# Gated units of a hybrid decoder block: gate and up of 2304 columns with the weights stationary and x moving

## Chip, core and metric

The kernel runs on one core of one Trainium2 chip. The metric is the time of one execution on the device, in microseconds. Three runs of the kernel before took 1052.83 us in the median (1052.79 to 1053.9). One more execution was recorded by the hardware profiler; its trace and its page are what the profile rows below come from.

## The reference

Two layers work on 256 tokens of 1024 columns in float32. Each layer has four sublayers, and each sublayer is normed before and after:

```python
for i in range(DEPTH):                       # 2
    f = swiglu(rmsnorm(h, g[0]), ffn_gate[i, 0], ffn_up[i, 0], ffn_down[i, 0])
    h = h + 0.5 * rmsnorm(f, g[1])
    mix = hybrid_mixer(rmsnorm(h, g[2]), ...)
    h = h + rmsnorm(mix, g[3])
    f = swiglu(rmsnorm(h, g[4]), ffn_gate[i, 1], ffn_up[i, 1], ffn_down[i, 1])
    h = h + 0.5 * rmsnorm(f, g[5])
    gate = jax.nn.sigmoid(rmsnorm(h, g[6]) @ w_ple_gate[i])
    h = h + rmsnorm((p[i] @ w_ple[i]) * gate, g[7])

def swiglu(x, w_gate, w_up, w_down):         # 1024 -> 2816 -> 1024
    return (jax.nn.silu(x @ w_gate) * (x @ w_up)) @ w_down
```

The change is in `swiglu`, which is computed four times. These are the four gated units; "unit 1" is the first of layer 0, "unit 2" the second of layer 0, and units 3 and 4 are those of layer 1.

## The kernel before

**Precision.** Every float32 operand of a product is split into two parts of 12 significant bits, hi and lo, and a product is three matmuls: hi by hi, hi by lo, lo by hi. For x the parts lie in `xh`, `xl`, transposed (columns of x on the partitions), one tile of each for each of the two token tiles t of 128 tokens.

**Weights.** The class `Weights` streams them in the order of their use. SP issues one load of 1 MB for each raw tile; there are four raw buffers, and the next load is issued when a raw tile is used up. A raw tile holds two pieces of 1024 columns. `prepare` splits a piece: ACT copies it to hi (L152), then DVE subtracts hi from the raw piece and writes lo (L153). There are ten slots for such pairs of hi and lo, two of them lent to the mixer while it runs. Where the splits stand among the other instructions is set by `PLAN`: `run` emits a phase of matmuls and, at the steps named there ("ticks"), one split each; other pieces of work are inserted at steps of their own. Every engine works in the order in which it is written here; the only planner is this table.

**A gated unit** (`ffn`) goes through the 2816 hidden columns in chunks of 512, 512, 256, 512, 512, 512. For a chunk there are six phases: gate of token tiles 0 and 1, up of 0 and 1, down of 0 and 1. In gate and up the parts of x are the stationary operand and the weights move, 512 columns at a time (L321 to L323), so tokens come out on the partitions, and the norm's factor of x, `rx`, is a number per partition. ACT makes the silu with that factor as its scale (L448). DVE makes (up times rx) times silu (L453). The product `hm` has tokens on the partitions, but down needs the hidden columns there: TensorE transposes four blocks of it (`hid_t`, L398), ACT copies the result to hi (L401) and DVE subtracts to lo (L402). Down (L479) then adds into four banks of PSUM that are kept for it (`accs`: two token tiles by two halves of the 1024 columns). All other products and transposes use a second pool of four banks in turn. In the last chunk the down phases go by halves of the columns, and `begin_post` and `post` form the norm of the result, which goes into the residual stream h and, normed and transposed, into x of the next sublayer.

**Beside this.** `setup_late` loads and builds masks and rotary tables for the mixer: four DMAs of SP from L292 on, a chain on DVE from L296 on, two sines on ACT (L308, L312). It is written once, behind the first chunk's down phases of unit 1. `extra` transposes the per-layer inputs p (`split_p`), in units 2 and 4, ahead of the last down phases.

Of the kernel before, what the change touches and what calls it, by code (L numbers as in the profile page):

```python
# [9 lines left out]
F32 = mybir.dt.float32  # L10
# [4 lines left out]
ALU = mybir.AluOpType  # L15
# [22 lines left out]
CHUNKS = [(0, 512), (512, 512), (1024, 256), (1280, 512), (1792, 512), (2304, 512)]  # L38
# [58 lines left out]
class Weights:  # L97
    """Streams the weights in the order of their use: one load per raw tile, which is then
    split into pieces hi + lo = w, each of 12 significant bits."""

    def __init__(self, nc, raw_pool, slots):
        """slots: pairs of (pool, tag, columns) for hi and lo; those of self.shut are taken by others."""
        self.nc, self.raw_pool, self.slots = nc, raw_pool, slots
        self.free = list(range(len(slots)))
        self.shut = set()
        self.slot = {}
        self.specs = []
        self.loads = []
        self.raw = {}
        self.got = {}  # L110
        self.next = 0
        self.next_load = 0

    def add(self, keys, src, a, n):
        load = len(self.loads)
        self.loads.append((src, a * len(keys), n))
        for i, key in enumerate(keys):
            self.specs.append((key, load, i, a, n, i == len(keys) - 1))
# [22 lines left out]
    def prepare(self):  # L141
# [3 lines left out]
        raw = self.raw[load][:, part * a : (part + 1) * a, :]  # L145
# [30 lines left out]
def hybrid_block(ctx: ExitStack, tc: tile.TileContext, a, out):  # L176
# [60 lines left out]
    for l in range(DEPTH):  # L237
        for f in range(2):
# [21 lines left out]
            for c, (f0, w) in enumerate(CHUNKS):  # L260
                ka = 1024 // w
                for name, src in (("G", wg), ("U", wu)):
                    for j in range(KD // (2 * ka)):
                        W.add([(l, f, c, name, 2 * j), (l, f, c, name, 2 * j + 1)],
                              src[:, 2 * ka * j : 2 * ka * (j + 1), f0 : f0 + w], ka, w)
                for j in range(w // 256):
                    k0 = f0 // P + 2 * j
                    W.add([(l, f, c, "D", 2 * j), (l, f, c, "D", 2 * j + 1)], wd[:, k0 : k0 + 2, :], 1, 1024)
# [20 lines left out]
    def setup_late():  # L289
        """Masks and rotary tables."""  # L290
# [25 lines left out]
    xh = [keep.tile([P, KD, P], F32R, name=f"xh{t}") for t in range(T)]  # L316
    xl = [keep.tile([P, KD, P], F32R, name=f"xl{t}") for t in range(T)]

# [6 lines left out]
    def run(gen, name, *fns):  # L325
        """Emits a phase of matmuls, with fns and splits of weights at the steps that PLAN has for it."""
# [15 lines left out]
    def rstd(ss, ns, tag="rs", eps=EPS):  # L342
        """(ss / n + eps) ** -0.5 for each column of ss."""
# [16 lines left out]
    def begin_post(t, f, gain, q):  # L360
        """For the first half of the columns: their part in f's norm, and f * gain. The norm's factor
        comes out divided by q."""
        e = sum_sq([f[0]])
        nc.gpsimd.tensor_scalar(e[:, 0:1], e[:, 0:1], q * q / D, q * q * EPS, op0=ALU.mult, op1=ALU.add)
        y = k2("y")
        nc.vector.tensor_tensor(y, f[0], gain[:, :512], op=ALU.mult)
        part[t] = e, y

    def post(t, f, gain, q, gain_pre):
        """h[t] += norm(f) / q; gives h[t] * gain_pre, and what does the second half of the columns."""  # L370
        e, y0 = part[t]
        r = rstd(sum_sq([f[1]]), [D / (q * q)], eps=e[:, 0:1])
        y1 = k2("y")
        nc.vector.tensor_tensor(y1, f[1], gain[:, 512:], op=ALU.mult)
# [32 lines left out]
    def proj(ps, t, keys, fin, cols=None, k0=0, first=True, last=True, sh=None, sl=None, lo_last=False):  # L407
        """ps += x[t] @ w over the pieces named by keys."""
# [24 lines left out]
    def ffn(l, f, pend, gain_post, gain_pre, extra=lambda: None):  # L433
        """pend: emits the transposes of x that are still to come. Gives the same for what follows."""
        hidden = work.tile([P, T, 2, 4, P], F32R, tag="k8", name="hid")
        hid = [(hidden[:, t, 0], hidden[:, t, 1]) for t in range(T)]
        sg = {}
        accs = {}

        def gkeys(c, name):  # L440
            return [(l, f, c, name, j) for j in range(4 if CHUNKS[c][1] == 512 else 2)]

        def gate(t, c, *fns, lo_last=False):
            w = CHUNKS[c][1]
            ps = bank("g")
            run(proj(ps[:, :w], t, gkeys(c, "G"), t == 1, lo_last=lo_last), f"{kind}.G{t}", *fns)
            s = k2("silu")
# [462 lines left out]
```

## Time and profile before

| | before |
|---|---|
| runs: median of three (lowest to highest) | 1052.83 us (1052.79 to 1053.9) |
| profiled execution, from the first to the last instruction | 1052.4 us |
| mean granted clock of TensorE (1 is full speed) | 0.999 |
| TensorE matmul busy | 1037.1 us |
| VectorE (DVE) busy | 645.8 us |
| ScalarE (ACT) busy | 528.9 us |
| GpSimd (POOL) busy | 51.1 us |
| DMA | 189.02 MB, mean 180 GB/s |

In the profile, PE is TensorE's matmul and PEld its weight load, SPq the queue of DMA issues of SyncE. A row of a timeline gives the start of a group of instructions in us from the span's start, its length, the engine, the line, the operation, the tiles (result, then sources), the shape, and how many instructions it holds; in brackets the idle time of the engine ahead of it and what ended that. A row of the costliest groups gives the number of instructions, their busy time, the mean ns of one, the engine's idle time ahead of them and its causes. Matmuls overlap in a trace, so the sum of their durations says less than the distance between two starts.

### The profile page before, as it was taken

The numbers are of one execution on the slowest core, as the hardware profiler recorded it, in microseconds if no ns is written. First come the engines' busy times: TensorE is split into PE (matmuls) and PEld (weight loads), VectorE is DVE, ScalarE is ACT, GpSimd is POOL, SyncE is SP. The second block draws the span as 40 slices with busy tenths as digits, with TensorE's granted clock in tenths as the row PEclk, the third lists the DMA queues.
The fourth block names the chain that finished last, engine by engine and source line by source line (L and its number), as shares of the span: only waits on it lengthen the run. The fifth ranks groups of instructions, "written<-read, shape, count | busy, mean of one in ns | idle before, by whom it ended". The sixth has DMA issues, their size and how long they took to land.

```text
span 1052.4 us, 13069 instructions
## 1 busy us (share of the span) xinstructions
PE 1037.1 (99%) x5168; PEld 867.0 (82%) x5168; DVE 645.8 (61%) x819; ACT 528.9 (50%) x744; POOL 51.1 (5%) x123
## 2 busy tenths in 40 slices
PE   8999999999999999999999999999999999999997
PEld 5889888878888898888878888888888888988886
DVE  4765554778677455456776545557877864555474
ACT  5544443555556444444665444445564654444463
POOL 0000000210020000000110000002000200000011
PEclk9999999999999999999999999999999999999999
DMA  8864546364227564554547645455532575545601
GB/s 321 304 227 168 193 164 211 106 222 160 82 94 272 191 213 160 201 200 160 200 160 259 212 169 200 153 163 168 180 120 82 190 275 184 198 162 172 227 21 40
DMA packets 86158, 189.02 MB, mean 180 GB/s; under 512 B 3665, under 2 KB 15313, under 8 KB 86098
## 3 DMA queue, kind: packets, MB, share of 16 engines
q1 hardware_dynamic: 86098, 188.20, 52.0%
q8 instruction: 40, 0.66, 0.2%
q14 instruction: 20, 0.16, 0.0%
HBM read 187.13 MB, written 1.05 MB: 179 GB/s over the span
## 4 chain that ended last, share of the span: by engine, by line
PE 92%; DVE 3%; ACT 2%; DMA 1%; issue 1%; POOL 0%; SPq 0%; DVEq 0%; POOLq 0%; ACTq 0%
PE acc L479 23%; PE u L323 8%; PE u L321 8%; PE u L322 8%; PE g L321 7%; PE g L323 7%; PE g L322 7%; PE tp L398 3%; PE o L706 2%; PE sc L666 1%; DVE lo L153 1%; PE gt L323 1%; PE gt L322 1%; PE gt L321 1%; PE f L321 1%; PE f L323 1%
## 5 line engine op out<-in xcount | busy, mean ns | idle before, releaser
L153 DVE TENSOR_TENSOR lo<-raw,hi 128x1024 fp32r<-128x1024 f32 (+1 forms) x338 | 405.1, 1214 | 204.2 <-ACT hi L152 194.1
L152 ACT ACTIVATE hi<-raw 128x1024 fp32r<-128x1024 f32 (+1 forms) x338 | 347.2, 1049 | 170.9 <-PE u L323 79.3
L479 PE MATMUL acc<-hi,hid 128*128 128x512 f32 x704 | 201.5, 392 | 0.0
L479 PEld LDWEIGHTS acc<-hi,hid 128*128 128x128 f32 x704 | 131.7, 188 | 27.4
L321 PE MATMUL u<-hi,xh 128*128 128x512 f32 (+1 forms) x384 | 145.3, 379 | 0.0
L323 PE MATMUL u<-hi,xl 128*128 128x512 f32 (+1 forms) x384 | 143.2, 373 | 0.0
L322 PE MATMUL u<-lo,xh 128*128 128x512 f32 (+1 forms) x384 | 143.0, 372 | 0.0
L321 PE MATMUL g<-hi,xh 128*128 128x512 f32 (+1 forms) x360 | 135.0, 375 | 2.3 <-ACT xh L401 2.3
L323 PE MATMUL g<-hi,xl 128*128 128x512 f32 (+1 forms) x360 | 134.6, 374 | 0.0
L322 PE MATMUL g<-lo,xh 128*128 128x512 f32 (+1 forms) x360 | 134.5, 374 | 0.0
L479 PE MATMUL acc<-lo,hid 128*128 128x512 f32 x352 | 118.3, 395 | 0.0
L323 PEld LDWEIGHTS u<-hi,xl 128*128 128x128 f32 x384 | 72.3, 188 | 13.0
L322 PEld LDWEIGHTS u<-lo,xh 128*128 128x128 f32 x384 | 72.4, 188 | 12.1
L321 PEld LDWEIGHTS u<-hi,xh 128*128 128x128 f32 x384 | 72.3, 188 | 12.0
L321 PEld LDWEIGHTS g<-hi,xh 128*128 128x128 f32 x360 | 68.5, 190 | 14.4 <-ACT xh L401 2.7
L322 PEld LDWEIGHTS g<-lo,xh 128*128 128x128 f32 x360 | 68.5, 190 | 12.3 <-DVE lo L153 0.5
L323 PEld LDWEIGHTS g<-hi,xl 128*128 128x128 f32 x360 | 68.4, 190 | 12.4 <-DVE xl L402 0.6
L479 PEld LDWEIGHTS acc<-lo,hid 128*128 128x128 f32 x352 | 66.2, 188 | 13.2
L401 ACT ACTIVATE hid<-tp 128x512 fp32r<-128x512 f32 (+1 forms) x48 | 27.0, 563 | 95.6 <-PE tp L398 95.6
L453 DVE SCALAR_TENSOR_TENSOR hm<-u,rs,silu 128x512 f32<-128x512 f32 (+1 forms) x48 | 33.7, 703 | 65.1 <-PE u L323 65.1
L448 ACT ACTIVATE silu<-g,rs 128x512 f32<-128x512 f32 (+1 forms) x48 | 31.3, 652 | 81.3 <-PE g L323 81.2
L402 DVE TENSOR_TENSOR hid<-tp,hid 128x512 fp32r<-128x512 f32 (+1 forms) x48 | 31.0, 647 | 44.0 <-ACT hid L401 43.6
(216 smaller groups left out, 1195.0 us busy)
## 6 DMA issues: line engine op xcount, KB each, us to landing
raw<-in_ffn_up SPq DMA_DIRECT2D x44, 1024.0 KB, 5.1
raw<-in_ffn_down SPq DMA_DIRECT2D x44, 1024.0 KB, 5.0
raw<-in_ffn_gate SPq DMA_DIRECT2D x43, 1024.0 KB, 5.2
raw<-in_w_in SPq DMA_DIRECT2D x12, 1024.0 KB, 5.2
raw<-in_w_out SPq DMA_DIRECT2D x8, 1024.0 KB, 5.1
raw<-in_w_ple_gate SPq DMA_DIRECT2D x8, 1024.0 KB, 5.1
gain<-in_norm_gains SPq DMA_DIRECT2D x15, 512.0 KB, 4.0
raw<-in_w_in SPq DMA_DIRECT2D x4, 832.0 KB, 5.2
```

Source lines behind the costliest of these rows:

```text
L152: self.nc.scalar.activation(hv, raw, AF.Copy)
L153: self.nc.vector.tensor_tensor(lv, raw, hv.bitcast(F32), op=ALU.subtract)
L321: nc.tensor.matmul(ps, sh, wh, start=first, stop=False)
L322: nc.tensor.matmul(ps, sh, wl, start=False, stop=False)
L323: nc.tensor.matmul(ps, sl, wh, start=False, stop=last)
L398: nc.tensor.transpose(ps[:, j * P : (j + 1) * P], src[:, (b0 + j) * P : (b0 + j + 1) * P], ident)
L401: nc.scalar.activation(hv, v, AF.Copy)
L402: nc.vector.tensor_tensor(dl[:, k0 + b0 : k0 + b0 + nb, :], v, hv.bitcast(F32), op=ALU.subtract)
L448: nc.scalar.activation(s[:, :w], ps[:, :w], AF.Silu, scale=rx[t][:, 0:1])
L453: nc.vector.scalar_tensor_tensor(hm[:, :w], ps[:, :w], rx[t][:, 0:1], sg[t][:, c0 : c0 + w], op0=ALU.mult, op1=ALU.mult)
L479: nc.tensor.matmul(accs[t][n], hid[t][x][:, b, :], ws[w][:, 0, n * 512 : (n + 1) * 512], start=first and x + w == 0, stop=final and x == 1)
L706: nc.tensor.matmul(dst, pt[:, b * P : (b + 1) * P], va[:, kb, hd, :], start=kb == 0, stop=kb == t)
```

## The change

The first 512 columns of each unit stay as they were, except that `hm` is now up times silu without `rx`. Both factors of x are left out on the up side; the post norm takes them in (`by`, through `times` and the scale of the sum of squares).

The other 2304 columns, 18 blocks (b = 4 to 21) of 128, are computed transposed. The four parts of x (hi of token tiles 0 and 1, lo of 0 and 1) become one tile `x4`, so that they can move as one row of 512 columns. `block` takes one block of weight columns: for each of the eight k tiles, the hi part of the weights is stationary and all of `x4` moves (512 columns), then the lo part is stationary and hi of x moves (256 columns). The first half of the bank then holds hi by hi plus lo by hi, the second hi by lo. `both` adds the halves: ACT copies the second to SBUF, DVE adds the first. The hidden columns are now on the partitions, as down needs them: the transposes of `hm` are gone in these blocks, and `rx` is a number per column there. `factors` spreads it over all partitions, once for each unit: two fills of ACT, two transposes of TensorE between the two down phases of the first 512 columns, one copy of ACT. DVE multiplies a gate block by these factors `rall`, ACT makes the silu; in an up block DVE multiplies by the silu, ACT copies to hi, and DVE subtracts to lo.

A raw tile of gate or up now holds two blocks, each with all eight k tiles (8 rows of 256 columns), and a split takes 128 of those 256 columns per row, still 1024 in all. The order is two gate blocks, two down blocks of the pair before, two up blocks, and so on; the first pair (4, 5) and the last (20, 21) have no down blocks between gate and up. The last four blocks go to down by the phases that were there before, by halves. Each phase of eight (or four) steps has a split at steps 1, 3, 5, 7. `setup_late` stays behind the first down phases.

```diff
-CHUNKS = [(0, 512), (512, 512), (1024, 256), (1280, 512), (1792, 512), (2304, 512)]
+NB = D_FF // P
...
+    "block": ((1, 3, 5, 7), ()),
+    "last.D0": ((1, 3, 5, 7), (4,)),
...
+            part = (slice(None), slice(None), slice(i * n, (i + 1) * n)) if cols else (slice(None), slice(i * a, (i + 1) * a))
...
+            for b in (0, 2):
+                pair("D", b)
+            for b in range(4, NB, 2):
+                pair("G", b)
+                if 4 < b < NB - 2:
+                    pair("D", b - 2)
+                pair("U", b)
+            for b in range(NB - 4, NB, 2):
+                pair("D", b)
...
+    x4 = keep.tile([P, KD, 2 * T, P], F32R, name="x4")
+    xh = [x4[:, :, t, :] for t in range(T)]
+    xl = [x4[:, :, T + t, :] for t in range(T)]
...
+            nc.vector.scalar_tensor_tensor(y, f, by, gain, op0=ALU.mult, op1=ALU.mult)
...
-            nc.vector.scalar_tensor_tensor(hm[:, :w], ps[:, :w], rx[t][:, 0:1], sg[t][:, c0 : c0 + w],
-                                           op0=ALU.mult, op1=ALU.mult)
+            nc.vector.tensor_tensor(hm, ps, sg[t], op=ALU.mult)
...
+        def factors():
+            ps = bank("rb")
+            for t in range(T):
+                b = k2("rxb")[:, :P]
+                nc.scalar.activation(b, ident, AF.Identity, scale=0.0, bias=rx[t][:, 0:1])
+                nc.tensor.transpose(ps[:, t * P : (t + 1) * P], b, ident)
+            r = work.tile([P, T * P], F32, tag="rall", name="rall")
+            nc.scalar.activation(r, ps[:, : T * P], AF.Copy)
+            return r
+
+        def block(ps, key):
+            wh, wl = W.need(key)
+            for k in range(KD):
+                hi = (ps, wh[:, k, :], x4[:, k].rearrange("p c q -> p (c q)"))
+                lo = (ps[:, : T * P], wl[:, k, :], x4[:, k, :T].rearrange("p c q -> p (c q)"))
+                for i, (o, w, x) in enumerate((hi, lo) if k < KD - 1 else (lo, hi)):
+                    nc.tensor.matmul(o, w, x, start=k + i == 0, stop=k == KD - 1 and i == 1)
+                yield
+            W.finish(key)
+
+        def both(ps, s):
+            nc.scalar.activation(s, ps[:, T * P :], AF.Copy)
+            nc.vector.tensor_tensor(s, ps[:, : T * P], s, op=ALU.add)
+
+        def gate_block(b, s):
+            ps = bank("g")
+            run(block(ps, (l, f, "G", b)), "block")
+            both(ps, s)
+            nc.vector.tensor_tensor(s, s, rall, op=ALU.mult)
+            nc.scalar.activation(s, s, AF.Silu)
+            sg[b] = s
+
+        def up_block(b, hb, s):
             ps = bank("u")
+            run(block(ps, (l, f, "U", b)), "block")
+            both(ps, s)
+            nc.vector.tensor_tensor(s, s, sg[b], op=ALU.mult)
+            nc.scalar.activation(hb[:, 0], s, AF.Copy)
+            nc.vector.tensor_tensor(hb[:, 1], s, hb[:, 0].bitcast(F32), op=ALU.subtract)
...
+        down(0, 0, False, lambda: hid_t(1, hm1))
+        rall = factors()
+        down(1, 0, False)
+        if kind == "start":
+            setup_late()
+        hbs = {}
+        for b in range(4, NB, 2):
+            if b == NB - 4:
+                hid8, hid = hidden()
+            gs, us = k2("gs"), k2("us")
+            for i in range(2):
+                gate_block(b + i, gs[:, i * T * P : (i + 1) * T * P])
+            if 4 < b < NB - 2:
+                for i in range(2):
+                    down_block(b - 2 + i, hbs[b - 2 + i])
+            for i in range(2):
+                if b < NB - 4:
+                    hbs[b + i] = k2("hb", F32R).rearrange("p (c q) -> p c q", c=2)
+                else:
+                    hbs[b + i] = hid8[:, b + i - (NB - 4)].rearrange("p c t q -> p c (t q)")
+                up_block(b + i, hbs[b + i], us[:, i * T * P : (i + 1) * T * P])
+        kind = "last"
+        extra()
+        by = [rx[t][:, 0:1] for t in range(T)]
+        down(0, NB - 4, True, lambda: begin_post(0, accs[0], gain_post, 2.0, by[0]))
```

What this makes of the instructions' order, at three places. First VectorE in unit 1, from the last instruction of the tables' setup on (`tab` is the rotary tables; `raw`, `hi`, `lo` are pieces of weights; `u`, `rs`, `silu`, `hm` up, the factor of x, silu and hidden). Before:

```order
L313 TENSOR_SCALAR tab_109<-tab_109 128x2x48
L153 TENSOR_TENSOR lo_475<-raw10_357,hi_474 128x1024
L153 TENSOR_TENSOR lo_514<-raw11_386,hi_513 128x1024
L153 TENSOR_TENSOR lo_524<-raw11_386,hi_523 128x1024
L153 TENSOR_TENSOR lo_536<-raw12_408,hi_535 128x1024
L453 SCALAR_TENSOR_TENSOR hm_569<-u_544,rs_201,silu_501 128x512
```

Now (`g` is the bank of a gate block, `gs` its sum in SBUF, `rall` the factors):

```order
L323 TENSOR_SCALAR tab_109<-tab_109 128x2x48
L152 TENSOR_TENSOR lo_482<-raw10_354,hi_481 128x1024
L508 TENSOR_TENSOR gs_476<-g_478,gs_476 128x256
L514 TENSOR_TENSOR gs_476<-gs_476,rall_405 128x256
L152 TENSOR_TENSOR lo_509<-raw11_383,hi_508 128x1024
L508 TENSOR_TENSOR gs_476<-g_505,gs_476 128x256
```

Before, four splits stood between the setup and the first instruction that frees a bank of TensorE; now one split does, and then each block has an add and a multiply between two splits.

Second, ScalarE in unit 1. Before, in the second chunk, from the silu of its second token tile on (`tp` is the bank of transposes, `hid` the transposed hidden columns):

```order
L448 ACTIVATE silu_542<-g_503,rs_206 128x512
L152 ACTIVATE hi_575<-raw12_408 128x1024
L152 ACTIVATE hi_587<-raw13_430 128x1024
L401 ACTIVATE hid_150<-tp_597 128x512
L152 ACTIVATE hi_604<-raw13_430 128x1024
L152 ACTIVATE hi_616<-raw14_478 128x1024
```

Now, from the first up block's copy to hi to the split after the next gate block's silu (`us` is an up block's sum, `hb` its hidden block):

```order
L523 ACTIVATE hb_530<-us_477 128x256
L151 ACTIVATE hi_563<-raw12_414 128x1024
L507 ACTIVATE us_477<-u_560 128x256
L523 ACTIVATE hb_559<-us_477 128x256
L151 ACTIVATE hi_591<-raw12_414 128x1024
L507 ACTIVATE gs_586<-g_588 128x256
L515 ACTIVATE gs_586<-gs_586 128x256
L151 ACTIVATE hi_618<-raw13_436 128x1024
```

Before, one instruction of 512 columns stood between two or more splits; now each block puts two of 256 columns ahead of each split, and the second of them follows DVE's multiply.

Third, TensorE at the start of the last down phase of unit 1 (`acc` is the bank of down; waits on semaphores in brackets). Before:

```order
L323 MATMUL u_1439<-hi_1313,xl1_113 128x512
L479 MATMUL acc00_346<-hi_1325,hid_150 128x512 [waits Activation_49]
L479 MATMUL acc00_346<-lo_1326,hid_150 128x512
L479 MATMUL acc00_346<-hi_1325,hid_150 128x512 [waits DVE_49]
L479 MATMUL acc00_346<-hi_1336,hid_150 128x512
L479 MATMUL acc00_346<-lo_1337,hid_150 128x512
```

Now, from the second matmul of the phase on:

```order
L555 MATMUL acc00_343<-lo_1484,hid_1450 128x512
L555 MATMUL acc00_343<-hi_1483,hid_1450 128x512
L555 MATMUL acc00_343<-hi_1508,hid_1450 128x512 [waits Activation_49]
L555 MATMUL acc00_343<-lo_1509,hid_1450 128x512
L555 MATMUL acc00_343<-hi_1508,hid_1450 128x512 [waits DVE_49]
L555 MATMUL acc00_343<-hi_1520,hid_1450 128x512 [waits Activation_49]
L555 MATMUL acc00_343<-lo_1521,hid_1450 128x512
L555 MATMUL acc00_343<-hi_1520,hid_1450 128x512 [waits DVE_49]
L555 MATMUL acc00_343<-hi_1536,hid_1450 128x512 [waits Activation_49]
L555 MATMUL acc00_343<-lo_1537,hid_1450 128x512
L555 MATMUL acc00_343<-hi_1536,hid_1450 128x512 [waits DVE_49]
```

Before, the phase waited for ACT and DVE once, for one transposed tile of four blocks; now it waits again for each of the blocks 19, 20 and 21, and the last of them is reached after nine matmuls.

More of the change, by code (lines that the diff above doesn't have):

```diff
@@ L144, in prepare @@
             self.load_one()
-        raw = self.raw[load][:, part * a : (part + 1) * a, :]
+        raw = self.raw[load][part]
         slot = self.pick()
@@ L433, in ffn @@
     def ffn(l, f, pend, gain_post, gain_pre, extra=lambda: None):
[L435 to L444, printed above, removed]
-            ps = bank("g")
-            run(proj(ps[:, :w], t, gkeys(c, "G"), t == 1, lo_last=lo_last), f"{kind}.G{t}", *fns)
-            s = k2("silu")
-            nc.scalar.activation(s[:, :w], ps[:, :w], AF.Silu, scale=rx[t][:, 0:1])
-            sg[t] = s
@@ L451, in mul, with hidden, keys, gate @@
-        def mul(t, ps, c0, w):
+        sg, accs = {}, {}
+        def hidden():
+            v = work.tile([P, 4, 2, T, P], F32R, tag="k8", name="hid")
+            return v, [(v[:, :, 0, t, :], v[:, :, 1, t, :]) for t in range(T)]
+        _, hid = hidden()
+        def keys(name):
+            return [(l, f, name, -1, j) for j in range(4)]
+        def gate(t, *fns, lo_last=False):
+            ps = bank("g")
+            run(proj(ps, t, keys("G"), t == 1, lo_last=lo_last), f"{kind}.G{t}", *fns)
+            sg[t] = k2("silu")
+            nc.scalar.activation(sg[t], ps, AF.Silu, scale=rx[t][:, 0:1])
@@ L463, in hid_t @@
[L463 to L468 removed]
+            nc.vector.tensor_tensor(hm, ps, sg[t], op=ALU.mult)
+            return hm
+        def hid_t(t, hm):
+            split_t(hm, 4, hid[t][0], hid[t][1])
+        def factors():
[7 more added lines that the diff above has]
+            return r
@@ new lines, in down_block, with gen @@
+        def down_block(b, hb):
+            def gen():
+                ws = W.need((l, f, "D", b))
+                for t in range(T):
+                    i = 0
+                    for x, w in ((0, 0), (0, 1), (1, 0)):
+                        for n in range(2):
+                            nc.tensor.matmul(accs[t][n], hb[:, x, t * P : (t + 1) * P], ws[w][:, 0, n * 512 : (n + 1) * 512],
+                                             start=False, stop=False)
+                            i += 1
+                            if i % 3 == 0:
+                                if t == 1 and i == 3:
+                                    W.finish((l, f, "D", b))
+                                yield
+            run(gen(), "block")
@@ L469, in down @@
+        def down(t, b0, end, *fns):
             halves = [[0], [1]] if end else [[0, 1]]
@@ L472, in gen @@
                 for ns in halves:
-                    for b in range(nb):
-                        ws = W.need((l, f, c, "D", b))
-                        first, final = c == 0 and b == 0, end and b == nb - 1
+                    for b in range(4):
+                        ws = W.need((l, f, "D", b0 + b))
+                        first, final = b0 + b == 0, end and b == 3
                         i = 0
@@ new lines, in ffn @@
+        kind = "first" if len(pend) == 3 else "start"
+        if kind == "first":
+            gate(0, pend[0], lo_last=True)
+            hm0 = up(0, pend[1], pend[2])
+            gate(1, lambda: hid_t(0, hm0))
+            hm1 = up(1)
+        else:
+            gate(0, *pend)
+            gate(1)
+            hm0 = up(0)
+            hm1 = up(1, lambda: hid_t(0, hm0))
+        accs.update({t: acc(f"acc{t}") for t in range(T)})
+        down(0, 0, False, lambda: hid_t(1, hm1))
+        rall = factors()
```

91 lines of the change are left out of this document (30 added, 61 removed), and 5 rows, old and new, of the table PLAN.

## The prediction

> **What bounds the kernel now.** I read the page first: busy times, then the chain that ended last.
>
> ```profile
> span 1052.4 us, 13069 instructions
> PE 1037.1 (99%) x5168; PEld 867.0 (82%) x5168; DVE 645.8 (61%) x819; ACT 528.9 (50%) x744; POOL 51.1 (5%) x123
> PE 92%; DVE 3%; ACT 2%; DMA 1%; issue 1%; POOL 0%; SPq 0%; DVEq 0%; POOLq 0%; ACTq 0%
> ```
>
> TensorE is the bound: 99% busy, 92% of the chain. VectorE (DVE) and ScalarE (ACT) have slack on average. The windows over the part that the change rewrites, from the second chunk's first gate matmul to the end of each of the four gated units, show it without a hole (columns: length, PE busy, PEld, DVE, ACT, POOL, clock):
>
> ```profile
> 48.15:200.79 152.64, 152.64 (x737) 128.01 (x736) 82.83 (x95) 66.88 (x81) 1.49 (x4) 1.00 0.55 187
> 346.40:499.60 153.20, 153.20 (x741) 128.45 (x740) 81.24 (x81) 68.25 (x80) 1.59 (x4) 1.00 0.55 186
> 565.22:717.85 152.63, 152.63 (x737) 128.00 (x736) 79.92 (x80) 67.01 (x79) 1.47 (x4) 1.00 0.53 178
> 862.90:1016.10 153.20, 153.20 (x742) 128.45 (x741) 81.25 (x81) 68.25 (x80) 1.59 (x4) 1.00 0.50 172
> ```
>
> So the question has two halves: what TensorE's own sum becomes, and whether DVE and ACT, which get more small work between their weight splits, still deliver in time.
>
> **TensorE's sum.** Matmuls overlap, so cost is the distance between starts. From the timeline of PE:
>
> ```profile
> 48.15 0.39 PE L321 MATMUL g<-hi,xh 128*128 128x512 f32 x1
> ...
> 59.03 0.39 PE L321 MATMUL u<-hi,xh 128*128 128x512 f32 x1
> ...
> 67.94 0.60 PE L398 MATMUL tp<-ident,hm 128*128 128x128 f32 x4
> ...
> 68.61 0.40 PE L322 MATMUL u<-lo,xh 128*128 128x512 f32 x1
> ...
> 81.84 0.28 PE L321 MATMUL g<-hi,xh 128*128 128x256 f32 x1
> ...
> 87.60 0.28 PE L321 MATMUL u<-hi,xh 128*128 128x256 f32 x1
> ```
>
> 48 matmuls of 512 columns take 10.88 us, 226.7 ns each; 48 of 256 columns 5.76 us, 120.0 ns. Halving the columns saves 106.7 ns, so 13.3 ns is fixed per matmul. Four transposes and one matmul take 0.67 us, so a group of four costs 0.44.
>
> The streamed columns do not change: before, a k-block of 128 weight columns takes three products for two token tiles, a quarter each of 512; now 512 + 256. The count does. Per unit, gate and up of the 18 blocks were 384 matmuls of 512 and 96 of 256 columns (98.6 us) and become 288 + 288 (99.85 us): +1.3 us. The transposes of 36 of those blocks' hidden tiles (two token tiles, 18 blocks) go, about 4 us. The new part: 36 blocks of 8 x 346.7 ns = 2.774 us, 14 down blocks of 12 matmuls (2.72 us each, 38.1), the last four down blocks 10.9, four transposes of x 0.45: 149.3 us against 152.64, **-3.4 us** per unit; with the four transposes of p in the second unit of each layer 149.7 against 153.20, **-3.5**. Weight loads stay hidden, since the 256-column run above loads before each matmul too (736 loads, 737 matmuls in the first window). The raw tiles of eight rows by 256 columns are also there before, in the third chunk, and PE never waits for one.
>
> The Trainium skill, page "TensorE: Matmul & The Clock Gate", section "Back-to-back issue gap", gives N/2.4 + 2.5 ns between warm matmuls, 216 and 109 ns here. The trace does not agree (226.7 and 120.0). By the page the 384 extra matmuls of all four units would cost 1.0 us and not 5.1, and the result would be 4 us lower.
>
> **The two factor transposes** stand between the two token tiles of the first down phase, and wait for two ACT fills that stand behind two weight splits. Rows of ACT, then of PE, in the first and third unit:
>
> ```profile
> 41.30 4.03 ACT L152 ACTIVATE hi<-raw 128x1024 fp32r<-128x1024 f32 x4
> ...
> 558.38 1.05 ACT L152 ACTIVATE hi<-raw 128x1024 fp32r<-128x1024 f32 x1
> ```
> ```profile
> 42.24 1.09 PE L479 MATMUL acc<-hi,hid 128*128 128x512 f32 x4
> ...
> 559.31 1.08 PE L479 MATMUL acc<-hi,hid 128*128 128x512 f32 x4
> ```
>
> Each row of four matmuls holds the phase's last two, so it ends at 42.24 + 0.45 = 42.7 and 559.8. The splits follow each other by 0.95, so the fills (128 columns, no row shows one: more than nothing and less than the 0.384 of 256 columns below, I take 0.3) come at 43.2 to 43.85 and 559.3 to 559.9. With two transposes and the way back to matmuls (0.3): **+1.5** in the first unit, **+0.5** in each of the others.
>
> **The loop between ACT and DVE.** Durations of the forms that the new blocks use, or the nearest:
>
> ```profile
> L153 DVE TENSOR_TENSOR lo<-raw,hi 128x1024 fp32r<-128x1024 f32 x326 | 393.5, 1222 | 199.1 <-ACT hi L152 189.2
> L152 ACT ACTIVATE hi<-raw 128x1024 fp32r<-128x1024 f32 x326 | 337.1, 1056 | 159.6 <-PE u L323 68.6 <-PE acc L479 59.2 <-PE g L323 22.3
> L448 ACT ACTIVATE silu<-g,rs 128x256 f32<-128x256 f32 x8 | 3.8, 473 | 8.8 <-PE g L323 8.8
> L402 DVE TENSOR_TENSOR hid<-tp,hid 128x256 fp32r<-128x256 f32 x8 | 3.4, 424 | 11.1 <-ACT hid L401 11.1
> L401 ACT ACTIVATE hid<-tp 128x256 fp32r<-128x256 f32 x8 | 3.1, 384 | 23.0 <-PE tp L398 23.0
> ```
> ```profile
> 119.61 0.60 ACT L401 ACTIVATE hid<-tp 128x512 fp32r<-128x512 f32 x1 [1.42 <-PE tp L398]
> 120.10 2.94 ACT L152 ACTIVATE hi<-raw 128x1024 fp32r<-128x1024 f32 x3
> ```
> ```profile
> 120.24 0.69 DVE L402 TENSOR_TENSOR hid<-tp,hid 128x512 fp32r<-128x512 f32 x1 [0.79 <-ACT hid L401]
> 121.19 2.36 DVE L153 TENSOR_TENSOR lo<-raw,hi 128x1024 fp32r<-128x1024 f32 x2 [0.26 <-ACT hi L152]
> ```
>
> Three splits of ACT in 2.94 follow by 0.95; two of DVE in 2.36 by 1.14: an instruction starts 0.10 (ACT) or 0.08 us (DVE) before the end of an independent one ahead. From ACT to DVE a result takes 0.03 (120.21 to 120.24); I use it for the other handovers too. Each engine works in written order, and the order ties them: in a gate block DVE's add and multiply, then ACT's silu, then ACT's split, then DVE's split, then DVE's add of the next block. That loop is 0.424 + 0.03 + 0.424 + 0.03 + (silu until ACT may go on, 0.28 to 0.37: as the copy or the silu row, less 0.10; I take the middle) + 1.056 + 0.03 + 1.14 = **3.46 us**. An up block has the same loop, with the copy to hi in the silu's place. TensorE needs 2.774 per block: the chain falls back 0.69 per block, by no lack of throughput. In a pair of down blocks it does two splits at 1.14 while TensorE takes 5.44, and wins 3.16 back. So four blocks and a pair change the lag by 4 x 0.69 - 3.16 = -0.40, but the first iteration (blocks 4 and 5) and the last (20 and 21) have no down pair.
>
> Who waits: a block's hidden hi is ready some 1.8 us after its last product plus the lag (copy, add, multiply, copy, handovers). In the middle its down block comes some 8 us after that product and hides lags up to 6. At the end nothing stands between: the last block's hi is needed after nine matmuls, 1.9 us after. The stall is the lag.
>
> - Units 2 and 4: lag 2.1 after the first four blocks, down to the floor 0.69 by block 19, then 4 x 0.69 more: 3.45, less 0.45 hidden by the transposes of p: **+3.0** each.
> - Unit 3: four of its last splits are of 832 columns, by the ratio 832/1024 of the two split rows 0.36 shorter per loop: 0.33 + 3 x 0.33 + 0.69: **+2.0**.
>
> **The first unit** differs: the tables' setup is written after its first down phases, ahead of the new blocks on DVE and ACT. Rows of SP, DVE and ACT:
>
> ```profile
> 48.60 0.57 SPq L292 DMA_DIRECT2D mask<-in_mask  x1
> ```
> ```profile
> 55.14 0.29 DVE L297 CAST mask<-mask 128x256 bf16<-128x256 f32 x1 [5.70 <-DMA mask<-in_mask]
> ```
> ```profile
> 58.91 0.28 ACT L312 ACTIVATE tab<-turns 128x96 f32<-128x96 f32 x1 [0.50 <-DVE turns L311]
> 59.10 1.04 ACT L152 ACTIVATE hi<-raw 128x1024 fp32r<-128x1024 f32 x1
> ```
>
> Before, nobody needed ACT or DVE from 48 to 59: the gate of 512 columns ran on one bank. Now four blocks of 2.774 fill the four banks in 11.1 us. The setup comes about 1.2 later, since the splits ahead of its DMAs wait for the later down phase: its end at 60.3, ACT's split, DVE's split, the first add at 62.5, done 62.9. TensorE, at the blocks from 42.7 + 1.5 + 5.44 = 49.6, wants the first bank again at 60.7: stall 2.2. The second bank comes at 62.5 + 3.46 + 0.42 = 66.4 against 65.7: 0.7. The hidden tiles of the first two down blocks come 1.35 after their adds (69.4, 72.9) against 69.2 and 73.5: 1.6 and 0.75. Together **+5.3**. The next adds follow at 76.4 and 79.8, and after two more splits the first up block's at 85.6, where its product, with the stalls, would let it start at 80.4: a lag of 5.2, with the second up block 5.9, less 6 x 0.40, and grows at the end as in unit 3 (-0.36 + 3 x 0.33 + 0.69): **+4.8**.
>
> At each unit's end the factor of x now enters the post norm; by the silu row against the copy row a factor per partition costs 0.09 per instruction, once on the way: between nothing and 0.2 us per unit, and I take nothing.
>
> The sum: unit 1 -3.4 + 1.5 + 5.3 + 4.8 = +8.2; unit 2 -3.5 + 0.5 + 3.0 = 0; unit 3 -3.4 + 0.5 + 2.0 = -0.9; unit 4 0. In all **+7.3 us** on the profiled span of 1052.4; the median of the runs, 1052.83, lies 0.4 above that span, so I forecast 1060.1 and say 1060.
>
> **The rivals.**
> 1. *ACT and DVE keep up* (faster). If the loop is at most 2.8 us, say because DVE waits less on ACT than I read from the order, only TensorE's sum and the factors are left: -13.8 + 3.0 = -10.8, 1042. It decides at a loop of 2.774. For it: DVE's new work is some 5 x 0.42 + 3 x 1.14 = 5.5 us per pair of gate and up blocks and one down block, which take TensorE 8.3. Against: the order is in series, and the setup's stall needs no loop at all.
> 2. *No change* (1051 to 1055): the loop at 3.3 and a setup that lands earlier by some us. The pieces are near their break-even, so this is no small case.
> 3. *The loop is 3.6 or more*: then a pair wins nothing back, lag stays, and each end costs 2 to 3 more, the first unit 5: 1070 and above. The bounds of silu and of the handovers alone move the loop by 0.05; rows that I cannot see (a split that reads 128 of 256 columns, an add with both sources on chip) could do more.
> 4. *TensorE's clock falls in the stalls.* The last row shows the clock after the last matmul (PE busy 0.00):
>
> ```profile
> 1046.00:1052.00 6.00, 0.00 (x0) 0.00 (x0) 2.20 (x4) 0.51 (x2) 0.81 (x2) 0.89 0.23 87
> ```
>
> Over 6 us without a matmul the mean is 0.89, so full clock held for most of it. My longest stall is two waits of some 2.5 us with matmuls between, and stays under that. Half clock for 3 us would add 1.5 us per stall, some 6 in all: 1066. The Trainium skill, page "TensorE: Matmul & The Clock Gate", section "HAM oscillation — how this bites in real kernels", warns of idle gaps over about 3.4 us, after which the clock is halved; the row above agrees that it falls in the end, and by the page a lag of 4.8 in one piece would cross it.
>
> **How the numbers follow.** Forecast and its own bounds (loop 3.37 to 3.55: 1055 to 1068) 0.56; rival 1 0.18; rival 2 0.09; rival 3 0.11; rival 4 0.06. The range leaves out most of rival 1 and the far part of 3: 1046 to 1072. A measurement of this kernel tells 0.2% (2.1 us) from no change. Faster by more: rival 1 and a rest, 0.20; within: 0.09; slower: 0.71.
>
> **What would show it.** Pairs of 346.7 ns in the blocks; no transposes of hidden tiles there; PE below 99%, its idle time ended by DVE's add (in the first unit, near 61 us) and by ACT's hi of the last hidden tile at each unit's end; DVE's split waiting for ACT's in each block, some 1.4 us. A PE without idle time in units 2 to 4, or a loop near 2.8, would prove me wrong; so would a matmul distance other than 227 and 120.

## The result, and the profile after

| | before | after |
|---|---|---|
| median of four runs (lowest to highest) | 1053.07 us (1052.79 to 1053.9) | 1067.27 us (1065.6 to 1069.05) |
| ratio, with its 95% interval | | 1.0136 (1.0121 to 1.0151) |
| span of the profiled execution | 1052.4 us | 1064.3 us |

The kernel became slower by 14.2 us; the forecast had said slower by 7. The sign and the places of the waits came out as forecast. The size did not, above all by one term of the sum. The page after the change:

```profile
span 1064.3 us, 14006 instructions
PE 1038.8 (98%) x5416; PEld 872.0 (82%) x5416; DVE 736.2 (69%) x1099; ACT 578.2 (54%) x964; POOL 51.1 (5%) x123
PE 82%; DVE 9%; ACT 5%; DMA 2%; issue 2%; SPq 0%; POOL 0%; DVEq 0%; POOLq 0%; ACTq 0%
```

TensorE is still 98% busy, but only 82% of the chain that ended last is its own. The windows of the four units, from the first new block to the unit's end (columns as before: length, PE, PEld, DVE, ACT, POOL, clock):

```profile
47.45:205.87 158.42, 152.91 (x797) 128.87 (x796) 104.88 (x165) 77.04 (x133) 1.66 (x4) 1.00 0.54 178
351.30:506.16 154.86, 152.38 (x802) 129.26 (x800) 103.83 (x151) 79.79 (x132) 1.84 (x4) 1.00 0.56 184
572.30:725.78 153.48, 151.94 (x798) 128.97 (x797) 102.32 (x150) 78.75 (x131) 1.37 (x4) 1.00 0.55 178
871.50:1027.96 156.46, 153.97 (x802) 130.44 (x801) 103.83 (x151) 79.81 (x132) 1.83 (x4) 0.99 0.50 168
```

Each is longer than before (152.64, 153.20, 152.63, 153.20), and the second column lies below the first: TensorE now waits. Where, the timeline of PE says (in brackets idle time and its cause); the first five rows are unit 1, the others the ends of units 1 to 4:

```profile
41.50 0.62 PE L490 MATMUL rb<-ident,rxb 128*128 128x128 f32 x2 [0.78 <-ACT rxb L489]
...
60.22 0.50 PE L502 MATMUL g<-x,hi 128*128 128x512 f32 x1 [1.34 <-DVE gs L508]
...
63.67 0.50 PE L502 MATMUL g<-x,hi 128*128 128x512 f32 x1 [0.37 <-DVE gs L508]
...
68.03 0.72 PE L533 MATMUL acc<-hi,hb 128*128 128x512 f32 x2 [1.30 <-ACT hb L523]
...
71.48 0.73 PE L533 MATMUL acc<-hi,hb 128*128 128x512 f32 x2 [0.39 <-ACT hb L523]
...
196.42 0.50 PE L555 MATMUL acc<-hi,hid 128*128 128x512 f32 x1 [2.10 <-ACT hid L523]
...
496.70 0.50 PE L555 MATMUL acc<-hi,hid 128*128 128x512 f32 x1 [2.48 <-ACT hid L523]
...
716.32 0.50 PE L555 MATMUL acc<-hi,hid 128*128 128x512 f32 x1 [1.54 <-ACT hid L523]
...
1016.90 0.50 PE L555 MATMUL acc<-hi,hid 128*128 128x512 f32 x1 [2.49 <-ACT hid L523]
```

These are the places that the forecast named: the factors, the four banks and the first hidden blocks behind the setup near 61 us, and the hi of the last hidden block at each end. A matmul's modelled end lies 0.16 us past the point where the next could start (0.39 long, 0.23 apart), so each gap costs 0.16 more than its bracket: 2.26, 2.65, 1.70 and 2.65 at the ends, 4.0 for the four in unit 1.

The loop between ACT and DVE, in DVE's timeline in unit 2:

```profile
484.97 0.41 DVE L508 TENSOR_TENSOR gs<-g,gs 128x256 f32<-128x256 f32 x1
485.42 0.42 DVE L514 TENSOR_TENSOR gs<-gs,rall 128x256 f32<-128x256 f32 x1
487.27 1.23 DVE L152 TENSOR_TENSOR lo<-raw,hi 128x1024 fp32r<-128x1024 f32 x1 [1.43 <-ACT hi L151]
488.42 0.42 DVE L508 TENSOR_TENSOR gs<-g,gs 128x256 f32<-128x256 f32 x1
```

From one add to the next 3.45 us, with 1.43 of it DVE waiting for ACT's half of the split. And TensorE's own step, from PE's timeline at the first matmul of each phase (two up blocks, two gate blocks, two down blocks, two up, two gate):

```profile
424.27 0.40 PE L502 MATMUL u<-x,hi 128*128 128x512 f32 x1
...
429.84 0.40 PE L502 MATMUL g<-x,hi 128*128 128x512 f32 x1
...
435.48 0.63 PE L533 MATMUL acc<-hi,hb 128*128 128x512 f32 x2
...
441.05 0.40 PE L502 MATMUL u<-x,hi 128*128 128x512 f32 x1
...
446.62 0.39 PE L502 MATMUL g<-x,hi 128*128 128x512 f32 x1
```

A pair of gate or up blocks takes 5.57 or 5.64 us where 5.55 was forecast, a pair of down blocks 5.57 where 5.44 was. No wait stands in these phases: the step itself is longer. This was in no row of before, and it is the largest error of the sum.

One thing more is in the windows of the 5 us behind each unit's end gap (the number ahead of the last two is the clock):

```profile
496.70:501.70 5.00, 5.00 (x22) 4.07 (x23) 3.37 (x5) 2.83 (x6) 0.81 (x2) 1.00 0.23 43
...
1016.90:1021.90 5.00, 5.00 (x15) 3.93 (x16) 2.98 (x4) 2.05 (x4) 0.55 (x1) 0.66 0.00 0
```

Both follow a gap of the same length. After the one TensorE goes on at full clock with 22 matmuls in 5 us; after the other the clock falls and 15 are done: 7 x 0.227 = 1.6 us lost. What sets the two apart is told with rival 4 below.

### The profile page after: what moved, and what is told of

Its sections match the earlier page's. It is cut to its first block, busy times and chain, and to the rows that moved or that the text cites. A ratio compares the mean times of both kernels' runs of the same rounds, so it can differ in the third digit from the quotient of the medians.

```text
span 1064.3 us, 14006 instructions
## 1 busy us (share of the span) xinstructions
PE 1038.8 (98%) x5416; PEld 872.0 (82%) x5416; DVE 736.2 (69%) x1099; ACT 578.2 (54%) x964; POOL 51.1 (5%) x123
## 4 chain that ended last, share of the span: by engine, by line
PE 82%; DVE 9%; ACT 5%; DMA 2%; issue 2%; SPq 0%; POOL 0%; DVEq 0%; POOLq 0%; ACTq 0%
PE g L502 15%; PE u L502 14%; PE acc L533 14%; PE acc L555 7%; DVE lo L152 4%; ACT hi L151 3%; PE o L792 2%; PE tp L415 2%; PE sc L752 1%; PE u L332 1%; PE u L334 1%; PE u L333 1%; PE f L332 1%; PE f L334 1%; PE f L333 1%
## 5 line engine op out<-in xcount | busy, mean ns | idle before, releaser
L151 ACT ACTIVATE hi<-raw 128x1024 fp32r<-128x1024 f32 (+1 forms) x338 | 345.0, 1042 | 17.2 <-PE acc L555 6.5
L502 PE MATMUL g<-x,hi 128*128 128x512 f32 x576 | 203.6, 397 | 1.7 <-DVE gs L508 1.7
L502 PE MATMUL u<-x,hi 128*128 128x512 f32 x576 | 202.4, 396 | 0.0
L502 PE MATMUL g<-x,lo 128*128 128x256 f32 x576 | 149.9, 281 | 0.0
L502 PE MATMUL u<-x,lo 128*128 128x256 f32 x576 | 149.4, 280 | 0.0
L533 PE MATMUL acc<-hi,hb 128*128 128x512 f32 x448 | 127.3, 395 | 1.7 <-ACT hb L523 1.7
L502 PEld LDWEIGHTS g<-x,hi 128*128 128x128 f32 x576 | 106.0, 188 | 22.0 <-DVE gs L508 2.3
L502 PEld LDWEIGHTS u<-x,hi 128*128 128x128 f32 x576 | 105.7, 188 | 20.4
L502 PEld LDWEIGHTS g<-x,lo 128*128 128x128 f32 x576 | 108.8, 189 | 6.6
L502 PEld LDWEIGHTS u<-x,lo 128*128 128x128 f32 x576 | 108.6, 188 | 6.6
L555 PE MATMUL acc<-hi,hid 128*128 128x512 f32 x256 | 80.0, 402 | 8.6 <-ACT hid L523 8.6
```

The lines of the kernel that those rows point to most:

```text
L151: self.nc.scalar.activation(hv, raw, AF.Copy)
L502: nc.tensor.matmul(o, w, x, start=k + i == 0, stop=k == KD - 1 and i == 1)
L533: nc.tensor.matmul(accs[t][n], hb[:, x, t * P : (t + 1) * P], ws[w][:, 0, n * 512 : (n + 1) * 512], start=False, stop=False)
L555: nc.tensor.matmul(accs[t][n], hid[t][x][:, b, :], ws[w][:, 0, n * 512 : (n + 1) * 512], start=first and x + w == 0, stop=final and x == 1)
```

## The experiments

Two questions: why is TensorE's step longer (theory A: turns between 512 and 256 columns; theory B: where the tiles lie in memory), and is the loop what makes the gaps. Runs 1, 2, 3 and 5 each change one thing in the changed kernel, run 6 stands on 2 and 3, run 7 puts four together, and run 8 stands on 7. Runs 4, 9 and 10 change the kernel before.

**1. One block's matmuls grouped by size.**

```diff
-            for k in range(KD):
-                for i, (o, w, x) in enumerate((hi, lo) if k < KD - 1 else (lo, hi)):
+            todo = his[:1] + los + his[1:]
+            for i, (o, w, x) in enumerate(todo):
```

> In each block of gate and up the matmuls are regrouped: one of 512 columns, the eight of 256, the other seven of 512, instead of 512 and 256 in turn. Nothing else changes. Theory A (the turns between 512 and 256 columns keep TensorE out of its even step): a pair of blocks takes 5.55 us instead of 5.57 to 5.64, 36 blocks 99.9 instead of 101.1 us, the time falls by 4 to 5 us. Theory B (it comes from elsewhere: where tiles lie in memory, or what the other engines do beside it): pairs stay at 5.57 to 5.64, the time within 1.5 us of the changed kernel.

1066.07 us (two runs, 1064.58 and 1067.55). PE's timeline in unit 2, at the same phases as above:

```profile
425.42 0.39 PE L502 MATMUL u<-x,hi 128*128 128x512 f32 x1
...
430.99 0.39 PE L502 MATMUL g<-x,hi 128*128 128x512 f32 x1
...
436.59 0.64 PE L534 MATMUL acc<-hi,hb 128*128 128x512 f32 x2
```

Pairs of 5.57 and 5.60. Over all 54 pairs of gate or up blocks in units 2 to 4 the mean is 5.59 instead of 5.62 us: about half of what lay above 5.55 is gone. The gain in time, 1.2 us, is within the spread of the runs; in the profiled one the clock fell after the gaps of units 2 and 4 both. Neither theory holds as it was put; run 6 settles it.

**2. The hidden blocks at another place.** The compiled program has the hidden blocks of the down blocks at byte 416 of 512, the weights at 288. Here their buffers are taken earlier, and lie at 288.

```diff
+    k2("hb", F32R)
+
     def bank(name, pool=None):
```

> The hidden blocks that the down blocks hold stationary lie at byte 416 of 512 in the changed kernel, all other operands at 288; here they are placed at 288 too. Theory B (the place of the stationary tile against the moving one sets the step): a pair of down blocks takes 5.44 to 5.47 us instead of 5.58, 0.9 us less per unit, 3 to 4 us in all, and if the uneven step is handed on to gate and up, up to 5 more. Theory A (turns of sizes): down pairs stay at 5.58 and the time within 1.5 us.

```profile
429.82 0.40 PE L504 MATMUL g<-x,hi 128*128 128x512 f32 x1
...
435.46 0.62 PE L535 MATMUL acc<-hi,hb 128*128 128x512 f32 x2
...
440.92 0.39 PE L504 MATMUL u<-x,hi 128*128 128x512 f32 x1
```

The down pair takes 5.46 (theory B, for down); the gate pair still 5.64, so no gain was handed on. The up pairs behind a down pair even went from 5.60 to 5.63 in the mean of 28, which takes back 1.0 of the 28 x 0.12 = 3.4 us that the down pairs gain. The two runs took 1066.4 and 1068.54, and show no gain in time: in the profiled one the clock fell after the gaps of units 2 and 4 both.

**3. The split ahead of silu and copy.** The loop is opened and nothing else.

```diff
-            nc.scalar.activation(s, s, AF.Silu)
+            later.append(lambda: nc.scalar.activation(s, s, AF.Silu))
...
-    "block": ((1, 3, 5, 7), ()),
+    "block": ((1, 3, 5, 7), (2,)),
```

What is in `later` (the up block's copy to hi and subtraction too) is emitted at step 2 of the next phase, behind its first split.

> ScalarE's silu (gate) and copy to hi (up) of a block are written behind the next weight split instead of ahead of it, so that VectorE's split no longer waits for VectorE's own multiply by way of ScalarE. No work is added or left out. My theory (a loop of 3.45 us per block against 2.8 on TensorE makes the lag and with it the four gaps at the units' ends): VectorE keeps 0.45 us behind each block, the gaps of 2.49, 2.88, 1.93 and 2.89 us fall below 0.8, no fall of the clock in unit 4, the stalls in unit 1 between 58 and 72 us shrink from 4.5 to about 2; in all -9 to -12 us, 1055 to 1058. Rival (the gap is the last block's own way through VectorE and ScalarE, which no order of splits shortens): gaps stay above 1.7, time within 3 us of the changed kernel.

1053.27 us over ten runs (1052.64 to 1055.62), 0.9995 of the kernel before (0.9984 to 1.0006): 14 us less than the changed kernel, level with the one before, and some 2 us below what was expected. Windows of its four units:

```profile
49.65:202.87 153.22, 152.00 (x797) 128.96 (x796) 106.40 (x165) 81.79 (x133) 1.66 (x4) 1.00 0.56 184
348.26:500.29 152.03, 152.03 (x801) 129.49 (x800) 106.20 (x151) 83.38 (x132) 1.72 (x4) 1.00 0.57 187
566.37:718.10 151.73, 151.73 (x797) 128.96 (x796) 104.34 (x150) 82.14 (x131) 1.37 (x4) 1.00 0.56 180
863.68:1015.72 152.04, 152.04 (x802) 129.50 (x800) 106.21 (x151) 83.37 (x132) 1.72 (x4) 1.00 0.53 173
```

In units 2 to 4 PE's busy time fills the window: no gap at any end. DVE and ACT do as much work as before the edit, so it was the order that cost, not the amount. What stands there, 151.7 to 152.0, is TensorE's own sum by itself, and it is 0.9 to 1.2 below the 152.63 and 153.20 of before, not 3.4. In unit 1 one gap is left, where the first bank waits for the setup.

**4. The kernel before, with its hidden tile moved by 128 bytes.** Pads of 128 bytes ahead of the tile and 384 behind it.

```diff
+        if (l, f) == (0, 0):
+            work.tile([P, 32], F32, tag="pad0", name="pad0")
         hidden = work.tile([P, T, 2, 4, P], F32R, tag="k8", name="hid")
+        if (l, f) == (0, 0):
+            work.tile([P, 96], F32, tag="pad1", name="pad1")
```

> The kernel before, with its tile of transposed hidden columns (the stationary operand of down) moved by 128 bytes, to byte 416 of 512; everything else stays where it was. Theory B: down phases of 48 matmuls and four transposes go from 11.4 us to about 11.6 (5 ns per matmul), 4 to 5 us in all. Theory A: within 0.5 us of the kernel before.

1057.39 us over seven runs, 1.0044 of the kernel before (1.0026 to 1.0062). Its groups of down (count, busy time, mean ns), and those of the kernel before behind them:

```profile
L483 PE MATMUL acc<-hi,hid 128*128 128x512 f32 x704 | 204.3, 396 | 0.0
...
L483 PE MATMUL acc<-lo,hid 128*128 128x512 f32 x352 | 119.4, 398 | 0.0
```
```profile
L479 PE MATMUL acc<-hi,hid 128*128 128x512 f32 x704 | 201.5, 392 | 0.0
...
L479 PE MATMUL acc<-lo,hid 128*128 128x512 f32 x352 | 118.3, 395 | 0.0
```

704 x 4 + 352 x 3 ns = 3.9 us, a little less than expected, and 3.8 is what the medians show. So the place alone does it, in a kernel that has none of the change.

**5. The setup's work later.** Its DMAs stay; DVE's and ACT's part comes after the down blocks of the iteration of block 12.

```diff
         if kind == "start":
-            setup_late()
+            setup_dma()
...
+            if b == 12 and kind == "start":
+                setup_late()
```

> Unit 1 only: the four DMAs of the tables' setup stay behind the first down phases, but the work of VectorE and ScalarE on them comes after the down blocks of the iteration of block 12, where the lag has room. Theory (the setup's wait for its DMAs holds the first add): first add 0.45 us behind its block instead of 9.3; the gaps of 1.73, 0.76, 1.70 and 0.79 us between 58 and 72 us go, -4.5 us there; the end of unit 1 has a gap of 2 to 3 us as before; the time falls by 3 to 5 us. Rival (the loop of 3.45 alone fills the four banks at the start): gaps of over 1 us in all stay between 58 and 72 us.

1064.02 us (two runs). In the changed kernel DVE waited for the setup's first DMA, and the first add came 9.3 us behind its block:

```profile
53.64 0.29 DVE L307 CAST mask<-mask 128x256 bf16<-128x256 f32 x1 [4.90 <-DMA mask<-in_mask]
...
59.75 0.42 DVE L508 TENSOR_TENSOR gs<-g,gs 128x256 f32<-128x256 f32 x1
```

Now it follows its block at once:

```profile
52.60 0.42 DVE L513 TENSOR_TENSOR gs<-g,gs 128x256 f32<-128x256 f32 x1 [0.91 <-ACT gs L512]
```

The window of unit 1 is 154.46 instead of 158.42, -4.0, with no idle time of TensorE over 0.45 us between 44 and 190 us. The end has its gap still (2.88 from start to start). The setup was the cause, as forecast.

**6. One size only.** The lo part of the weights moves all 512 columns too. The edits of runs 2 and 3 are in it as well; by themselves they left the pairs of gate and up at 5.64 and 5.62 us in the mean. The cut shows the rest.

```diff
-                lo = (ps[:, : T * P], wl[:, k, :], x4[:, k, :T].rearrange("p c q -> p (c q)"))
+                lo = (ps, wl[:, k, :], x4[:, k].rearrange("p c q -> p (c q)"))
```

> A measurement of the step, not a version: the lo part of the weights moves all of x4 too (512 columns), which adds the product lo by lo, so every matmul of a block has 512 columns; hidden blocks are placed at byte 288 and the splits written ahead of silu and copy, so that nothing else disturbs TensorE. Theory A (each turn between 512 and 256 columns costs a few ns): 16 matmuls of a block take 16 x 226.7 = 3.627 us, a pair 7.25, down pairs 5.44 to 5.46. Theory B (it is the weights as the stationary operand, whatever the sizes): the step is 230 or more, a pair 7.36 or more.

```profile
441.46 0.39 PE L504 MATMUL u<-x,hi 128*128 128x512 f32 x1
...
448.71 0.39 PE L504 MATMUL g<-x,hi 128*128 128x512 f32 x1
...
455.97 0.62 PE L545 MATMUL acc<-hi,hb 128*128 128x512 f32 x2
```

Pairs of 7.25 and 7.26, 226.7 ns per matmul: the step of before is back as soon as all have one size. So for gate and up it is theory A. Run 1 got half because each block still had a turn: by the starts of its matmuls the step is 228 to 236 ns for the five behind the eight of 256 columns, and 226 to 227 after that.

**7. Four parts together** (runs 1, 2, 3 and 5).

> Four of the changes together: matmuls of a block grouped by size, hidden blocks at byte 288, splits ahead of silu and copy, the setup's work after block 12. By the single runs: 1053.3 (splits ahead) less 2.4 (grouping: 72 pairs at 5.585 instead of 5.62), less 3.4 (28 down pairs at 5.46 instead of 5.58), less 1.6 (setup gap): 1046, 0.993 of the kernel before. If the parts share their gain: 1049.

1045.09 us over six runs (1044.54 to 1045.66), 0.9918 (0.9902 to 0.9933), where the single gains added up to 1046. The parts add up.

**8. Two blocks together, and the factors' fills ahead.** In all but the last two up blocks, two blocks share one run of each size.

```diff
+            for ps, (wh, wl) in zip(banks, ws):
+                todo += [(ps, wh[:, k, :], x4[:, k].rearrange("p c q -> p (c q)"), k == 0, False) for k in range(KD)]
+            for ps, (wh, wl) in zip(banks, ws):
+                todo += [(ps[:, : T * P], wl[:, k, :], x4[:, k, :T].rearrange("p c q -> p (c q)"), False, k == KD - 1)
+                         for k in range(KD)]
...
+        bs = fills()
         down(0, 0, False, lambda: hid_t(1, hm1))
-        rall = factors()
         down(1, 0, False)
+        rall = factors(bs)
```

> As the run with four parts; beside that two blocks are computed together (16 matmuls of 512 columns, then 16 of 256), which halves the turns of size, and the two fills for the factors are written ahead of the down phases, their transposes behind them. Theory A: a pair takes 5.565 instead of 5.585, 60 pairs, -1.2 us; the factor gaps of 1.17 us in unit 1 and some 0.3 in each other go, -2 us: 1043. Rival: two adds and two multiplies in a row bring the lag back at the units' ends, gaps of 0.5 to 1.5 us each: 1046 to 1048.

1041.20 us over five runs (1040.81 to 1041.95), 0.9882 (0.9862 to 0.9901), the fastest: 11.9 us below the kernel before, and 2 below what was expected. Units 1 and 2:

```profile
46.43:196.27 149.84, 149.84 (x799) 129.36 (x798) 102.83 (x165) 81.56 (x134) 1.65 (x4) 1.00 0.58 190
341.18:491.47 150.29, 150.29 (x803) 129.91 (x802) 101.43 (x151) 82.57 (x133) 1.69 (x4) 1.00 0.57 189
```

There is no gap in these units, nor in the other two, and TensorE's own sum stands at 149.84 and 150.29: the 149.3 and 149.7 of the forecast plus 0.5 to 0.6. The rival's lag did not come.

**9 and 10. Which places cost.** The kernel before again: everything moved by 128 bytes, and the hidden tile alone by 256 bytes.

```diff
+    const.tile([P, 32], F32, name="pad")
```
```diff
-            work.tile([P, 32], F32, tag="pad0", name="pad0")
+            work.tile([P, 64], F32, tag="pad0", name="pad0")
```

> The kernel before, with every tile behind the first few constants moved by 128 bytes, so that x, the weights and the hidden columns all lie at byte 416 of 512. If only the place of the stationary tile against the moving one counts: down's matmuls of hi by hidden keep their mean of 392 ns, gate and up theirs of 390 to 397, PE busy stays at 1037. If the place by itself counts (288 good, 416 bad): all of them rise by 4 to 6 ns, PE busy by 15 us or more.

> The kernel before, with the tile of transposed hidden columns moved by 256 bytes, to byte 32 of 512, everything else where it was. If any difference to the moving operand within 512 bytes costs: down's matmuls at 396 ns and 398 ns, as when it was moved by 128. If only a difference that is no multiple of 256 bytes costs: 392 and 395, as in the kernel before.

The groups of down in the one, then in the other:

```profile
L480 PE MATMUL acc<-hi,hid 128*128 128x512 f32 x704 | 201.5, 392 | 0.0
...
L480 PE MATMUL acc<-lo,hid 128*128 128x512 f32 x352 | 118.3, 395 | 0.0
```
```profile
L483 PE MATMUL acc<-hi,hid 128*128 128x512 f32 x704 | 201.5, 392 | 0.0
...
L483 PE MATMUL acc<-lo,hid 128*128 128x512 f32 x352 | 118.3, 395 | 0.0
```

Both are as in the kernel before (1053.39 and 1052.64 us, one run each). The place by itself costs nothing here, and 256 bytes between stationary and moving operand cost nothing; 128 bytes, in run 4, cost 3 to 4 ns per matmul.

## Why the prediction was right in kind and wrong in size

The sum of the forecast beside the profiled execution, in us on the span:

| term | forecast | measured |
|---|---|---|
| TensorE's own sum, four units | -13.8 | -3.4 |
| factors | +3.0 | +3.0 |
| setup in unit 1 | +5.3 | +4.0 |
| gaps at the four ends | +12.8 | +9.3 |
| fall of the clock | 0 | +1.6 |
| outside the change (start -2.1, first mixer -0.7, rest +0.2) | 0 | -2.6 |
| sum | +7.3 | +11.9 |

**The step that failed** is TensorE's sum: "36 blocks of 8 x 346.7 ns = 2.774 us, 14 down blocks of 12 matmuls (2.72 us each". The matmuls were counted right; their distance was taken from long runs of one size. Measured, a pair of blocks takes up to 5.64 and a down pair 5.57, which makes some 18 x 0.07 + 7 x 0.14 = 2.2 of the 2.6 us per unit that are missing; where the rest lies was not followed up. The four windows less their gaps and the fall of the clock are 152.12, 152.21, 151.78 and 152.21, 3.4 below before and not 13.8. Runs 6 and 1 show the turns of size as the cause in gate and up, runs 2 and 4 the place of the hidden blocks as the cause in down, and run 8 comes within 0.6 of the forecast sum where both are nearly gone. Rows of one size, 226.7 and 120.0, could not show either, and the forecast gave this term no range.

That the span misses by 4.6 us and not by these 10.4 is in part luck. Setup and gaps cost 4.8 less than forecast, and 2.6 came from outside the change, most of it at the start, where profiles differ anyway (see the base below); the fall of the clock took 1.6 the other way.

**The loop** was forecast at 3.46 and is 3.45; run 3 shows that it made the gaps. At the ends 3.0, 2.0 and 3.0 were forecast for units 2 to 4, and 2.65, 1.70 and 2.65 came. In unit 1, 4.8 was forecast and 2.26 came, and this is the failed step once more: a slower TensorE falls less far ahead, so the lag shrank by 0.7 per iteration (adds of the first up block 5.40, 4.67, 3.96, 3.27, 2.52, 1.75 us behind its last matmul, then 1.03) and not by the 0.40 of the forecast, which is 2.0 of the 2.5 us. A part of the missed term thus paid for itself.

**The setup** came where it was forecast; it cost 4.0, which run 5 confirms by taking 4.0 away. **The factors** cost what was forecast: the two first down phases of unit 1 took 47.45 - 34.61 = 12.84 us instead of 48.15 - 36.75 = 11.40, +1.4 for 1.5; those of the other units 11.9 instead of 11.4, +0.5 each.

**The rivals.** Rival 1 needed a loop of at most 2.8, rival 2 one of 3.3, and rival 3 one of at least 3.6; it is 3.45. With the loop opened, in run 3, the time is that of the kernel before and not the 1042 of rival 1, since its TensorE sum was the forecast's. Rival 4 is in part true, beside the forecast and not in its place: one fall of the clock, 1.6 us, as it had priced one stall, after a gap of 2.65 us. The Trainium skill, page "TensorE: Matmul & The Clock Gate", section "HAM oscillation — how this bites in real kernels", names gaps over about 3.4 us; the trace does not agree with it as a bound, since 2.65 was enough here.

The traces also show why gaps of one length differ. In all twelve profiles every change of the granted clock lies a whole multiple of 3.413 us behind its first rise to full speed. In the profile of the changed kernel the rise is at 14.02 us; the fall in unit 4 at 1017.54, the return at 1020.95 and the last fall at 1061.91 come 294, 295 and 307 times 3.413 us later. If each profile is cut into windows on this grid, 18 windows at full clock hold at most 1.46 us of busy PE (six of them behind these gaps, twelve at the ends of the kernels), and every one is followed by half clock; 3654 hold 1.55 us or more, and none is. The rows show the window with the gap of unit 4 and the next one, the second of the two windows that share the gap of unit 2 (the first holds 2.33 us), and then, from run 1, the window with most of the gap of unit 2 (the first number behind the comma is PE's busy time, the number ahead of the last two the clock):

```profile
1014.13:1017.54 3.41, 0.92 (x5) 0.48 (x4) 2.58 (x5) 1.59 (x5) 0.00 (x0) 1.00 0.00 0
1017.54:1020.95 3.41, 3.41 (x10) 2.67 (x10) 2.40 (x3) 1.41 (x3) 0.55 (x1) 0.50 0.00 0
...
495.30:498.71 3.41, 2.00 (x9) 1.59 (x10) 2.57 (x6) 2.48 (x5) 0.00 (x0) 1.00 0.35 137
```
```profile
493.83:497.24 3.41, 1.46 (x6) 0.67 (x4) 2.38 (x4) 1.64 (x3) 0.00 (x0) 1.00 0.88 293
```

The grid begins at another time in each profile (the first rise is at 12.90 to 16.43 us), so where a gap lies in it is chance, and with it whether 1.6 us are lost.

**The base.** The profiled execution of before was not a typical run. Each run's time lies 1.8 us above its span (1066.09 for 1064.3 here, and 1054.25 for 1052.4 in a run of before beside the experiments), so 1052.4 belongs to a run of some 1054.2, 1.4 above the median of 1052.83, and what lies around the span is 1.8 and not 0.4. One thing that varies from profile to profile is seen at the start, before and after:

```profile
10.17 0.79 PE L321 MATMUL g<-hi,xh 128*128 128x512 f32 x1 [2.28 <-ACT xh L401]
```
```profile
8.30 0.79 PE L332 MATMUL g<-hi,x 128*128 128x512 f32 x1 [0.26 <-ACT x L418]
```

The first matmul with weights waits 0.26 to 2.51 us in the profiles of these kernels, and this differs among kernels whose start is the same. So the miss of 7.2 us is 4.6 on the span (1064.3 for 1059.7), 1.4 from the base, and 1.2 because the median of the changed kernel lies above its profiled run.

The loss of 14 us is settled: run 3 takes back all of it by order alone. What stays open is why turns of size and a distance of 128 bytes cost time: the runs show that they do, and how much.

## What to carry to other kernels

Fewer matmul columns or transposes are worth their sum only if the rows that price them have the same pattern: the same sizes in turn, and operands at the same distance in memory. Where a change puts small work of two engines between splits, draw the order on both as a loop and compare it with what TensorE needs per block; here one instruction per block (in an up block two) written behind the split instead of ahead of it was worth 14 us. And a profiled span is one run: ask where it lies among the runs before a forecast is added to it.

## What the runs showed of the hardware that was not expected

- A matmul of 512 columns takes 226.7 ns in a run of its own size (run 6: 7.25 us for 32) and 228 to 236 for the five matmuls after eight of 256 columns (run 1). With the two in turn, 16 of each take 5.56 to 5.64 us instead of the 5.55 of even steps.
- A stationary tile 128 bytes off the moving operand's place within 256 bytes costs 3 to 4 ns per matmul of 512 columns (run 4: 396 and 398 ns of modelled duration for 392 and 395) and 5 ns in the down pairs of the changed kernel (5.58 for 5.46 us, 24 matmuls). Moving both, or one by 256 bytes, costs nothing.
- The granted clock changes only on a grid of 3.413 us, and it falls to half for the next 3.41 us when TensorE was busy for at most 1.46 us of a window; 1.55 us kept it at full speed. So a gap of 2.65 us cost nothing when at most 1.7 us of it lay in one window (unit 1 in three of three profiles, unit 2 in two of four), and half the clock for 3.41 us when 2.1 us or more did (unit 2 in two of four, unit 4 in four of four).
